# S5 rows ordered (input, place), and the input product's operand built on the vector engine from broadcast rows

## The chip, the cores and the metric

The kernel runs on one core of a Trainium2 chip. The metric is device time of one execution in microseconds (us); less is better. The engines of the core work side by side, each through its own queue in order: PE (TensorE, matrix products; its weight loads are listed as PEld), DVE (VectorE), ACT (ScalarE), POOL (GpSimd) and SP (SyncE), which here issues nearly all DMAs.

## The reference, cut to what matters

One layer with two kinds of heads in parallel, for a prompt of 256 positions and eight sample sequences of 8 positions, 320 columns in all. The part that the change touches is the S5 head group: 64 groups of 16 channels, each driving a 64-dimensional complex diagonal state.

```python
lam_bar = jnp.exp(lam_dt)
b_bar = ((lam_bar - 1.0) / lam)[..., None] * b
bu = jnp.einsum('nlgh,gph->lngp', ug, b_bar)
a = jnp.broadcast_to(lam_bar, (l, 1, S5_GROUPS, S5_STATE))
_, xs = lax.associative_scan(_lin_combine, (a, bu), axis=0)
y = jnp.einsum('lngp,ghp->nlgh', xs, c).real.reshape(n, l, S5_WIDTH)
y = y + d * uf
```

Around it stand the input projection (u, and q, k, v, g of eight retention heads), chunked retention with a per-head norm, a GLU on the S5 output, the output projection, and a SwiGLU feed-forward block with its norms.

## The kernel before

All activations are held transposed (features on partitions, 320 columns). Large products run in a helper `gemm` (L137): per 128-row step `k` three matmuls of 320 columns, high x high, high x low and low x high (L143 to L145), from weights that `wload` (L122) brings in slabs of eight steps: one DMA into `raw` on SP (L130), a cast to `hi` on ACT (L131), and `lo = raw - hi` on DVE (L133), three buffers of each.

The order on PE and POOL is written out by the program (`manual_schedule`, L924). DVE, ACT and SP are ordered by a planner: among what is ready it takes what was traced first, and a block under `high_priority(offset=...)` counts as that much earlier (weights 3000, evictions `EVAC` 1500). Each engine then works through its queue in order. Small work is woven between the projection's steps by generators: `clk.now` is a clock that counts 0.4 for each `k` step (L146), the given costs in `mm` (L101) and 0.12 for a transpose in `tr` (L105). A generator that says `yield DL["b1"]` goes on when the clock has moved that far (`run_due`, L91). The distances stand in `DL` (L918).

S5 runs in eight chunks `c` of eight groups. Chunk `c` starts at clock `T0 + PER * c` (L990, L920), chunk 0 out of the first head's value step (`head_v`, L748). A chunk handles four positions (`CH = 4`) at once, so one product takes rows (position in the block, channel). In `s5_chunk` (L583), in order:

- the chunk's columns `up_` go to DRAM (`via`) and come back as `kst`, whose 64-row halves are ordered (place, input channel): eight DMAs (L593 to L596);
- on DVE, `m1`, `m2` are B times the coefficients `gpc` (and C times `lpc`), then `bl` and `cl` are the real and imaginary combinations (L606 to L619), and the table `tb` (`s5_table`, L525);
- after `b1`: four transposes of `bl` on PE into a PSUM bank `pt` (L626 to L628), copied on ACT to `bst` (L630), and the load of the next but one chunk's B and C (`load_bc`, L547);
- after `b2`: the input product `pb` (32 matmuls, `bst` x `kst`, L639), the product `pk_` (16 matmuls), whose result goes to the last place of `toe`, and six DMAs that shift it to the other places (L650 to L653); then the scan on DVE (`s5_scan`, L552);
- after `scan`: the output product `py` (16 matmuls `toe` x `kst`, 32 `cl` x `xp`, L659 to L674), its eviction `ev`, one DMA to DRAM (`back`, L682) and eight back as `yc` (L684 to L687);
- after `y`: the D term and GELU on DVE and ACT, into `u32`.

`gpc` and `lpc`, the coefficients by chunk, are made once in `s5_powers` (L485) from `ff`, `gp` and `lp`, which `s5_params3` (L439) computes on DVE. In `head_v` the sample part of the values is copied twice on ACT, to `vsp` (L757, for the product of a pair of heads, L774) and to `vs` (L758), which goes to DRAM as `vd` (L1100) during the GLU product.

After the last projection (L1012) the program runs the remaining generators until chunk 7 is done (L1026), and then the products with `w_out` (`ps_o`), the GLU product (`ps_g`), again `w_out`, and the feed-forward block.

Of the kernel before, what the change touches and what calls it, by code (L numbers as in the profile page):

```python
# [12 lines left out]
F32 = mybir.dt.float32  # L13
# [19 lines left out]
CH = 4  # L33
NCP = NP // CH
NC = N // CH
# [6 lines left out]


@with_exitstack
def hybrid_kernel(ctx, tc, xT, w_in, w_in4, w_out, w_glu, w_fi, w_fo, vecs, s5p, bc, x0,
                  r0, trig, masks, kdec, kdf, gq,
                  yT, s5p_o, s5s_o, rp_o, rs_o):
    nc = tc.nc
    pe, act, dve, pool, sp = nc.tensor, nc.scalar, nc.vector, nc.gpsimd, nc.sync
# [18 lines left out]
    vd = drs.tile([H, NS, NB, P], F32, name="vd")  # L68
    voff = {}
    o = 0  # L70
# [30 lines left out]
    def mm(cost, *a, **k):  # L101
        pe.matmul(*a, **k)
        clk.now += cost

    def tr(out, in_):  # L105
        m = in_.shape[0]
        pe.transpose(out, in_, ident[:m, :m])
        clk.now += 0.12
# [68 lines left out]
    def tt(out, a, b, op):  # L177
        dve.tensor_tensor(out, a, b, op)  # L178
        return out
# [63 lines left out]
    def misc(name):  # L243
        return ps_m.tile([P, 512], F32, name=name, tag="misc", bufs=2)
# [8 lines left out]
    vs = mp.tile([64, H, P], F32, name="vs")  # L253
    gqt = mp.tile([P, H, NS], F32, name="gqt")
    retp = mp.tile([P, H, N], F32, name="retp")

# [2 lines left out]
        pool.memset(qgs[i], 0.0)  # L259

    smp = mp.tile([P, P], F32, name="smp")
    vsp = mp.tile([P, P], F32, name="vsp")
# [52 lines left out]
    gpc = s5.tile([P, 8, 2, 8, CH], F32, name="gpc")  # L315
    ecs = s5.tile([P, 2 * NE, NPAIR], F32, name="ecs")
    lx0 = s5.tile([P, 2, NPAIR, NB], F32, name="lx0")
    endp = s5.tile([P, 2, NPAIR], F32, name="endp")
    ends = s5.tile([P, 2, 2, NPAIR, NB], F32, name="ends")

# [164 lines left out]
    def s5_powers():  # L485
        for q in range(2):
            for d in range(2):
                o = lpc[:, :, q, 4 * d:4 * d + 4]
                act.mul(o, lp[:, q].rearrange("p e (c j) -> p c j e", j=4), -1.0 if d > q else 1.0)
                o = gpc[:, :, q, 4 * d:4 * d + 4]  # L490
                act.copy(o[:, :, :, 0], ff[:, q].rearrange("p (c j) -> p c j", j=4))
                act.copy(o[:, :, :, 1:], gp[:, q].rearrange("p e (c j) -> p c j e", j=4))

    def s5_turns(ec, es):
        pool.memset(e18[:, :, 0, :, 0:1], 1.0)
# [87 lines left out]
    def s5_chunk(c):  # L583
# [7 lines left out]
        sp.dma_start(via.rearrange("j g h s c -> (j g h) (s c)"), up_.rearrange("p s c -> p (s c)"))  # L591
        kst = s5.tile([P, 4, NC], F32, name="kst", tag="kst", bufs=2)
        for i in range(2):  # L593
            for e in range(CH):
                sp.dma_start(kst[64 * i + 16 * e:64 * i + 16 * e + 16],
                             via[2 * i:2 * i + 2, :, :, CH - 1 - e].rearrange("q g h c -> h (q g) c"))  # L596

        raw = raws[c]
        for q in range(2):
# [5 lines left out]
        shm = [P, 8, CH, 16]  # L605
        for w_, pc in ((0, gpc), (1, lpc)):  # L606
            m1, m2 = (s5.tile(shm, F32, name=f"m{q}", tag=f"m{q}", bufs=1) for q in range(2))
            b_ = raw[:, w_].unsqueeze(2).to_broadcast(shm)
            tt(m1, b_, pc[:, c, 0].unsqueeze(3).to_broadcast(shm), MUL)
            tt(m2, b_, pc[:, c, 1].unsqueeze(3).to_broadcast(shm), MUL)  # L610
            if w_ == 0:

                bl = s5.tile([P, 2, 2, 2, CH, 16], F32, name="bl", tag="bl", bufs=1)
                for r, (a, b, op) in enumerate(((m1[:, 0:4], m2[:, 4:8], SUB), (m1[:, 4:8], m2[:, 0:4], ADD))):
                    a, b = (t_.rearrange("p (u q) e h -> p u q (e h)", q=2) for t_ in (a, b))
                    tt(bl[:, r].rearrange("p q u e h -> p u q (e h)"), a, b, op)
# [5 lines left out]
        yield DL["b1"] + (4.0 if c == 0 else 0.0)  # L622
        if not c:
            tbl = s5_table(c)
        bst = s5.tile([P, 4, P], F32, name="bst", tag="bst", bufs=1)
        pt = misc("pt")  # L626
        for i in range(4):
            tr(pt[:, P * i:P * i + P], bl[:, i // 2, i % 2].rearrange("p u e h -> p (u e h)"))  # L628
        with tc.high_priority(offset=EVAC):
            act.copy(bst, pt.rearrange("p (i s) -> p i s", s=P))  # L630
        load_bc(c + 2)
        yield DL["b2"]
        pb = ps_b.tile([P, 2, 512], F32, name="pb", tag="pb", bufs=1)
        for i in range(4):
            for u in range(2):

                for g in range(2):
                    us, gs = slice(64 * u, 64 * u + 64), slice(64 * g, 64 * g + 64)
                    mm(0.04, pb[gs, u, NC * i:NC * i + NC], bst[us, i, gs], kst[us, 2 * (i % 2) + g],  # L639
                       start=True, stop=True, tile_position=(64 * u, 64 * g))  # L640
        pk_ = misc("pk_")
        for i in range(2):
            for q in range(2):
                for u in range(2):
                    mm(0.04, pk_[64 * u:64 * u + 64, 32 * i:32 * i + 32],
                       bl[:, q, i, u].rearrange("p e h -> p (e h)"), cl0[:, q, 2 * u + i],
                       start=q == 0, stop=q == 1, tile_position=(0, 64 * u))
        with tc.high_priority(offset=EVAC):
            act.copy(toe[:, :, CH - 1], pk_[:, 0:64].rearrange("p (q h) -> p q h", h=16))
        for u in range(2):  # L650
            for t in range(CH - 1):
                d = 16 * (CH - 1 - t)
                sp.dma_start(toe[64 * u + d:64 * u + 64, :, t], toe[64 * u:64 * u + 64 - d, :, CH - 1])  # L653
        with tc.high_priority(offset=2 * EVAC if c == 7 else 0):
            s5_scan(c, pb, xp, d0, tbl)
        yield DL["scan"]
# [21 lines left out]
            tt(ev, ev,  # L678
               py[:, :, 2 * NC:4 * NC].rearrange("p g (u c) -> p u g c", c=NC), ADD)

        back = drm.tile([2, CH, 16, 2, 2, NC], F32, name="back", tag="back", bufs=2)
        sp.dma_start(back.rearrange("i t h u g c -> (i t h) (u g c)"), ev.rearrange("p u g c -> p (u g c)"))  # L682
        yc = s5.tile([P, CH, NC], F32, name="yc", tag="yc", bufs=1)
        for j in range(4):  # L684
            for g in range(2):
                r = 32 * j + 16 * g
                sp.dma_start(yc[r:r + 16], back[j % 2, :, :, j // 2, g].rearrange("t h c -> h t c"))  # L687
# [60 lines left out]
    def head_v(h, v_, qg, rt, R):  # L748
# [22 lines left out]
        nt = 2 + h % 2  # L771
        if h % 2:
            two = (HS[h - 1], R)
            mm(0.22, po[:, 2], smp, vsp, start=True, stop=False, skip_group_check=True)  # L774
# [133 lines left out]
    def do_g(h):  # L908
        ps = proj(11 + 4 * h)
        sg = mp.tile([P, N], F32, name="sg", tag="sg", bufs=2)  # L910
        with tc.high_priority(offset=EVAC):
# [337 lines left out]
def _host(inp):  # L1249
# [36 lines left out]
    A["bc"] = c(np.stack([np.concatenate([pairs(p + q, p == "s5_c_") for q in ("re", "im")], 2)  # L1286
                          for p in ("s5_b_", "s5_c_")], 2))
    x0 = np.stack([g("state_s5_re")[0], g("state_s5_im")[0]], 0)
    A["x0"] = c(x0.reshape(2, NB, NPAIR, P).transpose(3, 0, 2, 1))
    A["r0"] = c(g("state_ret")[0].transpose(1, 2, 0, 3))  # L1290
# [53 lines left out]
```

## Time and profile before

| | |
|---|---|
| time, median of 3 runs | 1434.91 us (1433.25 to 1435.58) |
| the profiled execution | 1433.95 us, its span 1432.1 us |
| TensorE clock granted | 0.997 |
| ACT, DVE, POOL busy | 598.8, 954.6, 125.1 us |
| DMA | 101803 packets, 266.87 MB, mean 186 GB/s |

The page of the profile gives busy time by engine, then groups of instructions by line, with the number, the mean duration of one, and the idle time of the engine ahead of them. A timeline row is start, duration, engine, line, operation, tiles written and read, and in brackets the idle time before it and what ended it. The duration of a PE matmul overlaps with the next one's, so the distance between two starts is read beside it. SPq rows are DMA issues: their duration is that of the issue, and the landing comes later.

### The profile page before, as it was taken

The page shows a single profiled execution, that of the slowest core. Times are in us where ns is not written, and L with a number is a line of the kernel's source. Part 1 is how long each engine was busy: PE and PEld are TensorE (multiplying, and loading weights), DVE is VectorE, ACT ScalarE, POOL GpSimd, SP SyncE. Part 2 cuts the span into 40 slices and gives each one's busy share as a digit, 9 for nine tenths or more (in the row PEclk, how much of TensorE's full clock was granted, in tenths as well). Part 3 has the DMA queues.
Part 4 walks back from the last instruction along what each step waited for, and adds up shares of the span by engine and source line. Part 5 has one row for each costly group of instructions (what it writes and reads, how often), then busy time and mean ns, then how long its engine had stood idle before and what let it go on. Part 6 is the DMA issues. An engine that isn't in the chain of part 4 may idle for free.

```text
span 1432.1 us, 26209 instructions
## 1 busy us (share of the span) xinstructions
PE 1418.1 (99%) x10394; PEld 1407.6 (98%) x10394; DVE 954.6 (67%) x1853; ACT 598.8 (42%) x944; POOL 125.1 (9%) x193
## 2 busy tenths in 40 slices
PE   9999999999999999999999999999999999999996
PEld 9999999999999999999999999999999999999996
DVE  7978887777567647776677546777644767644554
ACT  7645555554355433333333333333333333333452
POOL 7530022110000010000001000001000000000001
PEclk9999999999999999999999999999999999999998
DMA  8555555556544466675666446757445765444442
GB/s 285 175 172 161 165 167 165 169 160 208 162 156 152 152 210 228 221 250 205 239 217 228 128 150 234 247 202 254 151 152 185 256 225 183 153 127 156 148 148 108
DMA packets 101803, 266.87 MB, mean 186 GB/s; under 512 B 27312, under 2 KB 41776, under 8 KB 101680
## 3 DMA queue, kind: packets, MB, share of 16 engines
q1 hardware_dynamic: 101536, 264.94, 55.7%
q8 instruction: 81, 1.33, 0.4%
q14 instruction: 42, 0.34, 0.1%
q10 hardware_dynamic: 144, 0.26, 0.1%
HBM read 254.24 MB, written 10.52 MB: 185 GB/s over the span
## 4 chain that ended last, share of the span: by engine, by line
PE 71%; DVE 1%; issue 0%; ACT 0%; DVEq 0%
PE ps_fu L144 7%; PE ps_fu L143 7%; PE ps_fo L143 7%; PE ps_fo L144 7%; PE ps_fo L145 7%; PE ps_fu L145 7%; PE ps_fg L144 7%; PE ps_fg L143 7%; PE ps_fg L145 7%; PE ps_o L145 1%; PE ps_o L143 1%; PE ps_o L144 1%; PE ps_g L144 1%; PE ps_g L145 1%; PE ps_g L143 1%; DVE x L178 0%
## 5 line engine op out<-in xcount | busy, mean ns | idle before, releaser
L131 ACT CAST hi<-raw 128x1024 fp32r<-128x1024 f32 (+1 forms) x416 | 402.2, 968 | 697.4 <-PE ps_fo L144 189.0
L133 DVE TENSOR_TENSOR lo<-raw,hi 128x1024 fp32r<-128x1024 f32 (+1 forms) x416 | 467.5, 1124 | 314.9 <-ACT hi L131 312.4
L144 PE MATMUL ps_fo<-alo,hi 128*128 128x320 f32 x704 | 217.5, 309 | 0.0
L143 PE MATMUL ps_fg<-hhi,hi 128*128 128x320 f32 x704 | 217.5, 309 | 0.0
L143 PE MATMUL ps_fo<-ahi,hi 128*128 128x320 f32 x704 | 217.5, 309 | 0.0
L145 PE MATMUL ps_fo<-ahi,lo 128*128 128x320 f32 x704 | 217.5, 309 | 0.0
L144 PE MATMUL ps_fu<-hlo,hi 128*128 128x320 f32 x704 | 217.4, 309 | 0.0
L145 PE MATMUL ps_fg<-hhi,lo 128*128 128x320 f32 x704 | 217.4, 309 | 0.0
L143 PE MATMUL ps_fu<-hhi,hi 128*128 128x320 f32 x704 | 217.4, 309 | 0.0
L144 PE MATMUL ps_fg<-hlo,hi 128*128 128x320 f32 x704 | 217.4, 309 | 0.0
L145 PE MATMUL ps_fu<-hhi,lo 128*128 128x320 f32 x704 | 217.4, 309 | 0.0
L143 PE MATMUL ps_p<-xhi,hi 128*128 128x320 f32 x560 | 177.3, 317 | 0.0
L145 PE MATMUL ps_p<-xhi,lo 128*128 128x320 f32 x560 | 173.0, 309 | 0.0
L144 PE MATMUL ps_p<-xlo,hi 128*128 128x320 f32 x560 | 172.8, 309 | 0.0
L144 PEld LDWEIGHTS ps_fg<-hlo,hi 128*128 128x128 f32 x704 | 132.4, 188 | 0.0
L143 PEld LDWEIGHTS ps_fo<-ahi,hi 128*128 128x128 f32 x704 | 132.4, 188 | 0.0
L143 PEld LDWEIGHTS ps_fu<-hhi,hi 128*128 128x128 f32 x704 | 132.4, 188 | 0.0
L144 PEld LDWEIGHTS ps_fu<-hlo,hi 128*128 128x128 f32 x704 | 132.4, 188 | 0.0
L145 PEld LDWEIGHTS ps_fo<-ahi,lo 128*128 128x128 f32 x704 | 132.4, 188 | 0.0
L145 PEld LDWEIGHTS ps_fu<-hhi,lo 128*128 128x128 f32 x704 | 132.4, 188 | 0.0
L143 PEld LDWEIGHTS ps_fg<-hhi,hi 128*128 128x128 f32 x704 | 132.3, 188 | 0.0
L145 PEld LDWEIGHTS ps_fg<-hhi,lo 128*128 128x128 f32 x704 | 132.3, 188 | 0.0
(441 smaller groups left out, 2066.6 us busy)
## 6 DMA issues: line engine op xcount, KB each, us to landing
raw<-w_fi SPq DMA_DIRECT2D x176, 512.0 KB, 4.1
raw<-w_in SPq DMA_DIRECT2D x79, 512.0 KB, 4.1
raw<-w_fo SPq DMA_DIRECT2D x64, 512.0 KB, 3.5
raw<-w_out SPq DMA_DIRECT2D x32, 512.0 KB, 3.7
hi<-vd SPq DMA_DIRECT2D x32, 512.0 KB, 5.5
lo<-vd SPq DMA_DIRECT2D x32, 512.0 KB, 5.2
raw<-w_fo SPq DMA_DIRECT2D x64, 192.0 KB, 2.4
rt<-r SPq DMA_DIRECT2D x8, 512.0 KB, 5.3
```

The costliest lines, as they stand in the source:

```text
L131: cast = act.copy(hi[:, :m], raw[:, :m])
L133: last_lo[0] = dve.tensor_tensor(lo[:, :m], raw[:, :m], f(hi[:, :m]), SUB)
L143: pe.matmul(ps, hi, xhi[:, k], start=k == 0, stop=False)
L144: pe.matmul(ps, hi, xlo[:, k], start=False, stop=False)
L145: pe.matmul(ps, lo, xhi[:, k], start=False, stop=k == nk - 1)
```

## The change

Rows of the S5 operands are ordered (input channel, place) in place of (place, input channel). With that order `kst` comes from DRAM in two DMAs of 64 rows, `yc` in four of 32 rows, and `back` is written in four; `toe` is shifted by six DMAs over every fourth partition.

The transposed operand of the input product is no longer made by transposing `bl`. The host passes B already in rows, once for each of the four places (`bt`). A new generator `s5_rows` copies the coefficients into `gs` (eight ACT copies), transposes them once (two PE transposes), and writes them to DRAM (`gtd`). For each chunk `load_rows` loads `btr` (256 KB) and, broadcast over the 16 inputs, `gtr` (two DMAs of 128 KB), and `s5_bst` multiplies them on DVE: six operations of 128x256. `bl` stays, for `pk_`. `load_rows(c + 1)` stands behind chunk `c`'s `pb`.

`vs` gets the pair layout of `vsp`, which goes; `vd` is written by sixteen DMAs in place of eight.

```diff
@@ s5_powers
-                o = gpc[:, :, q, 4 * d:4 * d + 4]
-                act.copy(o[:, :, :, 0], ff[:, q].rearrange("p (c j) -> p c j", j=4))
-                act.copy(o[:, :, :, 1:], gp[:, q].rearrange("p e (c j) -> p c j e", j=4))
+            for e in range(CH):
+                src = gp[:, q, e - 1] if e else ff[:, q]
+                act.copy(gpc[:, :, q, :, CH - 1 - e].rearrange("p c (d j) -> p c d j", j=4),
+                         src.rearrange("p (c j) -> p c j", j=4).unsqueeze(2).to_broadcast([P, 8, 2, 4]))
+
+    def s5_rows():
+
+        gs = s5.tile([P, 2, 2, CH, 8, 2], F32, name="gs", tag="bl", bufs=1)
+        for r in range(2):
+            for e in range(CH):
+                src = gp[:, r, e - 1] if e else ff[:, r]
+                act.copy(gs[:, r, :, CH - 1 - e], src.rearrange("p (c u q) -> p u c q", u=2, q=2))
+        yield DL["rows"]
+        pt = misc("pt")
+        for r in range(2):
+            tr(pt[:, P * r:P * r + P], gs[:, r].rearrange("p u e c q -> p (u e c q)"))
+        gt = s5.tile([P, 2, P], F32, name="gt", tag="gtr", bufs=1)
+        with tc.high_priority(offset=EVAC):
+            act.copy(gt, pt[:, 0:2 * P].rearrange("p (r s) -> p r s", s=P))
+        sp.dma_start(gtd.rearrange("u e c q r s -> (u e c q) (r s)"), gt.rearrange("p r s -> p (r s)"))
+        load_rows(0)
+
+    rows = {}
+
+    def load_rows(c):
+        if c < 8:
+            b, g = (s5.tile([P, 2, 2, P], F32, name=n, tag=n, bufs=1) for n in ("btr", "gtr"))
+            sp.dma_start(b, bt[c])
+            for u in range(2):
+                sp.dma_start(g[64 * u:64 * u + 64].rearrange("p q r s -> p (q r s)"),
+                             gtd[u, :, c].rearrange("e q r s -> e (q r s)").unsqueeze(0)
+                             .to_broadcast([16, CH, 4 * P]))
+            rows[c] = b, g
+
+    def s5_bst(c):
+        b, g = rows.pop(c)
+        t_ = s5.tile([P, 2, 2, P], F32, name="bt_", tag="m0", bufs=1)
+        for r in range(2):
+            tt(t_[:, :, r], b[:, :, 1 - r], g[:, :, 1], MUL)
+        for r in range(2):
+            tt(b[:, :, r], b[:, :, r], g[:, :, 0], MUL)
+            tt(b[:, :, r], b[:, :, r], t_[:, :, r], ADD if r else SUB)
+        return b
@@ s5_chunk
-            for e in range(CH):
-                sp.dma_start(kst[64 * i + 16 * e:64 * i + 16 * e + 16],
-                             via[2 * i:2 * i + 2, :, :, CH - 1 - e].rearrange("q g h c -> h (q g) c"))
+            sp.dma_start(kst[64 * i:64 * i + 64], via[2 * i:2 * i + 2].rearrange("q g h s c -> (h s) (q g) c"))
...
-        bst = s5.tile([P, 4, P], F32, name="bst", tag="bst", bufs=1)
-        pt = misc("pt")
-        for i in range(4):
-            tr(pt[:, P * i:P * i + P], bl[:, i // 2, i % 2].rearrange("p u e h -> p (u e h)"))
-        with tc.high_priority(offset=EVAC):
-            act.copy(bst, pt.rearrange("p (i s) -> p i s", s=P))
+        bst = s5_bst(c).rearrange("p q r s -> p r q s")
         load_bc(c + 2)
         yield DL["b2"]
...
+        load_rows(c + 1)
...
-        for u in range(2):
-            for t in range(CH - 1):
-                d = 16 * (CH - 1 - t)
-                sp.dma_start(toe[64 * u + d:64 * u + 64, :, t], toe[64 * u:64 * u + 64 - d, :, CH - 1])
+        for t in range(CH - 1):
+            for i in range(t + 1):
+                sp.dma_start(toe[i::CH, :, t], toe[i + CH - 1 - t::CH, :, CH - 1])
...
-        back = drm.tile([2, CH, 16, 2, 2, NC], F32, name="back", tag="back", bufs=2)
-        sp.dma_start(back.rearrange("i t h u g c -> (i t h) (u g c)"), ev.rearrange("p u g c -> p (u g c)"))
+        back = drm.tile([2, CH, 2, 2, 16, NC], F32, name="back", tag="back", bufs=2)
+        for u in range(2):
+            for g in range(2):
+                sp.dma_start(back[:, :, u, g].rearrange("i t h c -> (i t) h c"), ev[:, u, g])
         yc = s5.tile([P, CH, NC], F32, name="yc", tag="yc", bufs=1)
         for j in range(4):
-            for g in range(2):
-                r = 32 * j + 16 * g
-                sp.dma_start(yc[r:r + 16], back[j % 2, :, :, j // 2, g].rearrange("t h c -> h t c"))
+            sp.dma_start(yc[32 * j:32 * j + 32], back[j % 2, :, j // 2].rearrange("t g h c -> (g h) t c"))
@@ head_v
-        act.copy(vsp[64 * (h % 2):64 * (h % 2) + 64], vT[64:128, 2])
-        last = act.copy(vs[:, h], vT[64:128, 2])
+        last = act.copy(vs[64 * (h % 2):64 * (h % 2) + 64, h // 2], vT[64:128, 2])
         if h == 0:
             rot_t["values"] = last
             with tc.issue_after(last.ins):
                 s5_powers()
+                spawn(s5_rows())
             start_chunk(0)
@@ DL
-    DL = dict(b1=14.2, b2=6.6, scan=17.8, y=10.0, k=8.5, v=6.1,
+    DL = dict(b1=14.2, b2=6.6, scan=17.8, y=10.0, rows=11.0, k=8.5, v=6.1,
@@ the GLU product
-            sp.dma_start(vd[:, :, n].rearrange("h t e -> t h e"), vs[NS * n:NS * n + NS])
+            for g in range(2):
+                sp.dma_start(vd[g::2, :, n].rearrange("h t e -> t h e"), vs[64 * g + NS * n:64 * g + NS * n + NS])
```

More of the change, by code (lines that the diff above doesn't have):

```diff
@@ L44, in hybrid_kernel @@
 @with_exitstack
-def hybrid_kernel(ctx, tc, xT, w_in, w_in4, w_out, w_glu, w_fi, w_fo, vecs, s5p, bc, x0,
+def hybrid_kernel(ctx, tc, xT, w_in, w_in4, w_out, w_glu, w_fi, w_fo, vecs, s5p, bc, bt, x0,
                   r0, trig, masks, kdec, kdf, gq,
@@ L261, in hybrid_kernel @@
     smp = mp.tile([P, P], F32, name="smp")
-    vsp = mp.tile([P, P], F32, name="vsp")
     qsp = mp.tile([P, P], F32, name="qsp")
@@ L317, in hybrid_kernel @@
     lx0 = s5.tile([P, 2, NPAIR, NB], F32, name="lx0")
+    gtd = drm.tile([2, CH, 8, 2, 2, P], F32, name="gtd", tag="gtd", bufs=1)
     endp = s5.tile([P, 2, NPAIR], F32, name="endp")
@@ L604, in s5_chunk @@
             act.copy(d0[:, :, :, 1:], r4[:, js].unsqueeze(1).unsqueeze(3).to_broadcast([P, 2, 4, NCP - 1]))
-        shm = [P, 8, CH, 16]
         for w_, pc in ((0, gpc), (1, lpc)):
+            dm = 3 - w_
+            shm = [P, 8, CH, 16] if w_ else [P, 8, 16, CH]
             m1, m2 = (s5.tile(shm, F32, name=f"m{q}", tag=f"m{q}", bufs=1) for q in range(2))
-            b_ = raw[:, w_].unsqueeze(2).to_broadcast(shm)
-            tt(m1, b_, pc[:, c, 0].unsqueeze(3).to_broadcast(shm), MUL)
-            tt(m2, b_, pc[:, c, 1].unsqueeze(3).to_broadcast(shm), MUL)
+            b_ = raw[:, w_].unsqueeze(dm).to_broadcast(shm)
+            tt(m1, b_, pc[:, c, 0].unsqueeze(5 - dm).to_broadcast(shm), MUL)
+            tt(m2, b_, pc[:, c, 1].unsqueeze(5 - dm).to_broadcast(shm), MUL)
             if w_ == 0:
-                bl = s5.tile([P, 2, 2, 2, CH, 16], F32, name="bl", tag="bl", bufs=1)
+                bl = s5.tile([P, 2, 2, 2, 16, CH], F32, name="bl", tag="bl", bufs=1)
                 for r, (a, b, op) in enumerate(((m1[:, 0:4], m2[:, 4:8], SUB), (m1[:, 4:8], m2[:, 0:4], ADD))):
-                    a, b = (t_.rearrange("p (u q) e h -> p u q (e h)", q=2) for t_ in (a, b))
-                    tt(bl[:, r].rearrange("p q u e h -> p u q (e h)"), a, b, op)
+                    a, b = (t_.rearrange("p (u q) h s -> p u q (h s)", q=2) for t_ in (a, b))
+                    tt(bl[:, r].rearrange("p q u h s -> p u q (h s)"), a, b, op)
                 continue
@@ L638, in s5_chunk @@
                     us, gs = slice(64 * u, 64 * u + 64), slice(64 * g, 64 * g + 64)
-                    mm(0.04, pb[gs, u, NC * i:NC * i + NC], bst[us, i, gs], kst[us, 2 * (i % 2) + g],
+                    mm(0.04, pb[gs, u, NC * i:NC * i + NC], bst[us, i // 2, i % 2, gs], kst[us, 2 * (i % 2) + g],
                        start=True, stop=True, tile_position=(64 * u, 64 * g))
+        load_rows(c + 1)
         pk_ = misc("pk_")
@@ L773, in head_v @@
             two = (HS[h - 1], R)
-            mm(0.22, po[:, 2], smp, vsp, start=True, stop=False, skip_group_check=True)
+            mm(0.22, po[:, 2], smp, vs[:, h // 2], start=True, stop=False, skip_group_check=True)
             for j in range(4):
@@ L1287, in _host @@
                           for p in ("s5_b_", "s5_c_")], 2))
+    bt = np.stack([pairs("s5_b_" + q, False) for q in ("re", "im")], 0)
+    bt = bt.reshape(2, P, 8, 2, 2, 16).transpose(2, 3, 5, 4, 0, 1)
+    A["bt"] = c(np.broadcast_to(bt[:, :, :, None], (8, 2, 16, CH, 2, 2, P)).reshape(8, P, 2, 2, P))
     x0 = np.stack([g("state_s5_re")[0], g("state_s5_im")[0]], 0)
```

4 lines of the change are left out of this document (2 added, 2 removed).

## The prediction

> **What bounds the kernel now.** The first view is the page's table of busy time, then the same shares over the stretch in which the S5 chunks run.
>
> ```profile
> span 1432.1 us, 26209 instructions
> ...
> PE 1418.1 (99%) x10394; PEld 1407.6 (98%) x10394; DVE 954.6 (67%) x1853; ACT 598.8 (42%) x944; POOL 125.1 (9%) x193
> ```
>
> ```profile
> 43.50:341.90 298.40, 297.87 (x2750) 290.90 (x2748) 243.12 (x516) 162.48 (x360) 63.23 (x114) 1.00 0.52 161
> ```
>
> The columns of the second are stretch, length, then busy us and instructions of PE, PEld, DVE, ACT and POOL, granted clock, DMA share and GB/s. From the first projection after the norm to the last, PE stands still for 298.40 - 297.87 = 0.53 us. DVE has 55.3 us left there, ACT 136. So an instruction taken off PE is worth its slot, and one put on DVE is free until PE has to wait for it. What PE waited for is the third view.
>
> ```profile
> PE py L102 <- DMA toe<-toe: 0.5, 1, 0.5
> ...
> PE pss L102 <- POOL ksp L886: 0.5, 1, 0.5
> PE ps_g L144 <- DVE ylo L182: 0.3, 1, 0.3
> ```
>
> Columns: total us, times, longest. No wait is for `kst` or `yc`: fewer DMAs as such can win back only the 0.5 us of `toe`.
>
> **Off PE: 32 transposes.** The timeline of PE around chunk 0's four, and their group:
>
> ```profile
> 78.29 0.31 PE L145 MATMUL ps_p<-xhi,lo 128*128 128x320 f32 x1
> 78.44 0.60 PE L107 MATMUL pt<-ident,bl 128*128 128x128 f32 x4
> 78.79 0.39 PE L143 MATMUL ps_p<-xhi,hi 128*128 128x320 f32 x1
> 79.03 0.30 PE L144 MATMUL ps_p<-xlo,hi 128*128 128x320 f32 x1
> ```
>
> ```profile
> L107 PE MATMUL pt<-ident,bl 128*128 128x128 f32 x32 | 4.8, 272 | 0.0
> ```
>
> Instructions overlap, so the price is the distance of starts. The next projection matmul begins 78.79 - 78.44 = 0.35 us after the first transpose, and the one after it follows 0.24 us later instead of the usual 0.15, which costs 0.09 more. One group is 0.44 us, eight are 3.5. `s5_rows` puts two transposes back: one start distance of (0.60 - 0.272) / 3 = 0.11, a short one and the 0.09, about 0.2. **Net on PE: -3.3 us.** The products `pb`, `pk` and `py` keep their number and shapes.
>
> The Trainium skill ("TensorE: Matmul & The Clock Gate", Part 4: PE-mode transpose) gives about 275 ns for a transpose inside a kernel and says that access latency dominates it. The group's mean of 272 ns agrees as a duration; the start of the next matmul after 0.35 us for four does not agree as a price.
>
> **Onto DVE: six operations of 128x256 a chunk. Off ACT: the copy of `bst`.** Nearest rows, in the views by form:
>
> ```profile
> L178 DVE TENSOR_TENSOR bl<-m,m 128x256 f32<-128x256 f32 x16 | 6.2, 420 | 0.2
> ```
>
> ```profile
> L630 ACT COPY bst<-pt 128x512 f32<-128x512 f32 x8 | 4.7, 588 | 0.4 <-PE pt L107 0.4
> ...
> L492 ACT COPY gpc<-gp 128x96 f32<-128x96 f32 x4 | 0.9, 299 | 0.0
> ```
>
> DVE gets 6 x 0.42 = 2.5 us a chunk, 20.2 in all, against 55.3 idle. ACT loses 4.7 us and the eight copies into `vsp`, and gains eight copies of 32 elements into `gs` (each under the 299 ns of the 96-element copy) and one of `gt`: a gain on an engine with 136 us to spare, worth nothing. In chunks 1 to 7 `btr` and `gtr` are ordered right behind the previous chunk's `pb`, some 33 us ahead, and the six operations follow `tb`, which is done ahead of its chunk's transposes; there I price the new wait of `pb` at nothing. The cover is the 6.6 units of the planner between the old transposes and `pb` (8.5 us in chunk 0, 78.44 to 86.96); without it a chunk would cost up to 2.5 us. Bounds for the 20.2 us of DVE work: nothing, or 20.2 if none were hidden; I take nothing outside chunk 0, since the idle time is the nearer row. The reordered products `m`, `bl` keep shapes and counts; their new strides I take at 0, by the rows of the same shape.
>
> **DMAs.** Per chunk `kst` goes from 8 to 2, `yc` from 8 to 4, `back` from 1 to 4, `toe` stays at 6, and three loads (256 + 2 x 128 KB) come in: 25 become 21.
>
> ```profile
> kst<-via SPq DMA_DIRECT2D x64, 20.0 KB, 3.4
> back<-ev SPq DMA_DIRECT2D x8, 160.0 KB, 3.6
> yc<-back SPq DMA_DIRECT2D x64, 20.0 KB, 3.5
> raw_bc<-bc SPq DMA_DIRECT2D x8, 128.0 KB, 3.7
> ```
>
> ```profile
> L595 SPq DMA_DIRECT2D kst<-via x64: 306/424/1315, 47.8 to 319.2; - x64
> ```
>
> ```profile
> L653 SPq DMA_DIRECT2D toe<-toe x48: 585/597/1404, 88.7 to 340.7; - x48
> ```
>
> The first fence ends in us to landing, the other two give ns of issue (least, median, most). SP saves 10 issues of about 0.42 us and pays 3 more `back` and 3 loads, so some 1.7 us a chunk, if the larger `kst` issues at the same price (at the 0.6 of `toe` still 1.3). No wait of PE hangs on it, except at two places.
>
> **Place 1, chunk 7's second product.** PE's order is fixed in the program: `py` of chunk 7 stands right behind the last projection and ahead of the `w_out` products.
>
> ```profile
> 330.04 0.78 PE L102 MATMUL pb<-kst,bst 64*64 64x80 f32 x32
> ```
>
> ```profile
> 341.95 0.36 PE L102 MATMUL py<-kst,toe 64*64 64x80 f32 x4
> 342.80 0.43 PE L102 MATMUL py<-kst,toe 64*64 64x80 f32 x10 [0.50 <-DMA toe<-toe]
> ```
>
> ```profile
> 332.34 1.37 SPq L687 DMA_DIRECT2D yc<-back  x3
> 333.80 1.88 SPq L653 DMA_DIRECT2D toe<-toe  x3
> 338.29 0.36 SPq L130 DMA_DIRECT2D raw<-w_out  x1
> 338.75 2.54 SPq L653 DMA_DIRECT2D toe<-toe  x3
> ```
>
> ```profile
> 337.04 1.22 DVE L133 TENSOR_TENSOR lo<-raw,hi 128x1024 fp32r<-128x1024 f32 x1
> 338.18 0.75 DVE L178 TENSOR_TENSOR xp<-v,v 128x252 f32<-128x252 f32 x2
> ```
>
> Chunks start at fixed readings of the planner's clock, which counts 0.4 for a projection step that takes 0.44 us. Without 3.1 units of transposes by then, 8 to 9 more steps fit ahead of `pb`(7): it moves to about 330.7, while the last projection ends 3.3 us earlier and PE reaches `py` at 338.65. The distance that hid the scan and `toe` shrinks from 11.9 to 8.0 us. `xp` is ready 8.9 us after `pb` (338.93), so at 339.6: PE reaches the products that read it near 339.1 and waits 0.5, as long as before. `toe`: half of its DMAs stood behind a weight load that waited for `lo` until 338.26, and three `yc` stood ahead of it. Now `yc` has 4 DMAs and `kst`(7) only 2, so `yc`(6) should be through before `toe` is ready near 332.4. Six issues of 0.6 end at 336.3; with the last landing about 1.5 us behind its issue (342.80 against 338.75 + 2.54) that is 337.8, in time. I take a wait of 0.5 us here, change 0; bounds: -0.5 and +4.0 (rival A).
>
> **Place 2, chunk 0's operand**, which needs the coefficient rows through DRAM first.
>
> ```profile
> 54.29 0.55 PE L107 MATMUL pst<-ident,v__743 128*128 128x128 f32 x3
> ```
>
> ```profile
> 64.75 0.91 ACT L492 COPY gpc<-gp 128x96 f32<-128x96 f32 x4
> ```
>
> ```profile
> 70.06 0.35 SPq L130 DMA_DIRECT2D raw<-w_in  x1
> ...
> 73.46 0.33 SPq L130 DMA_DIRECT2D raw<-w_in  x1
> ...
> 78.87 6.05 SPq L130 DMA_DIRECT2D raw<-w_in  x3
> ```
>
> ```profile
> 76.95 0.76 DVE L178 TENSOR_TENSOR tb<-e,e 128x256 f32<-128x256 f32 x2
> ...
> 80.64 1.75 DVE L133 TENSOR_TENSOR lo<-raw,hi 128x1024 fp32r<-128x1024 f32 x1
> 83.09 1.48 DVE L133 TENSOR_TENSOR lo<-raw,hi 128x1024 fp32r<-128x1024 f32 x1 [0.69 <-ACT hi L131]
> 86.19 0.42 DVE L178 TENSOR_TENSOR sm<-pss,mk 128x256 f32<-128x256 f32 x1 [1.62 <-PE pss L102]
> ```
>
> ```profile
> 86.96 0.78 PE L102 MATMUL pb<-kst,bst 64*64 64x80 f32 x32
> ```
>
> The rows' two transposes stand 11 units behind head 0's value transposes: 11 / 0.4 x 0.44 = 12.1 us and some products of the head, so near 68. Their input `gs` comes after the `gpc` copies, near 67: a wait of PE of 0 to 1.5 us, I take 0. Then a copy, `gtd` out (landing 3.6 as `back`) and `gtr` in (3.7 as `raw_bc`), each behind a weight load: about 69.5, 73.5, 77.5. The six operations then have 9 us, in which DVE is idle for 0.69 + 1.62 us and has 2.5 to do: `pb`(0) is late by 0.2, which I take.
>
> The sum: -3.3 + 0 + 0.2 = **-3.1 us**, so a profiled execution of 1433.95 - 3.1 = 1430.9 with a span near 1429.0 (1.9 us lie around the span). That execution lies 0.96 below the median of the three runs; against the median it is 1434.9 - 3.1 = **1431.8 us**. About 0.2%, 2.9 us, is what a measurement of this kernel can tell from no change, so the forecast lies just beyond it.
>
> **Rivals.**
>
> A. *The end of the projections is bound by chunk 7, not by PE.* If a weight load splits `toe` as before, its last half lands at 342.80 + 0.7 = 343.5 while PE is at `py` from 338.65; after the first products it waits 4.5 us instead of 0.5. Sum: -3.3 + 4.0 = +0.7, **1435.6**. For it: the split and the shrunken distance; against: the fewer DMAs ahead. Chance 0.22.
>
> B. *The rows come late, slower than before.* DVE works in order: a `bst` operation that waits for `gtr` holds the `lo` of the weights behind it. If `gtr` is issued behind the three weight loads that keep SP from 78.87 to 84.92, it lands near 88.5; 2.5 us of products, with a `lo` of 1.22 between, bring `pb`(0) to 92.5 instead of 86.96, and the held `lo` adds about 1: +6.5 in all, **1438.1**. It decides from rows landing after 83, and costs more than it wins from about 86. For it: DVE is full here, and `lo` took 1.75 and 1.48 instead of 1.22 while Pool worked. Chance 0.13.
>
> The Trainium skill ("SBUF — State Buffer", SBUF: two separate sides) says that a DVE instruction with two SBUF inputs and a GpSimd instruction that reads SBUF exclude each other for the whole instruction. All six operations have two SBUF inputs; the `lo` of 1.75 us agrees in direction, and by it the 2.5 us would be 3.6 (x 1.75 / 1.22), by the rule more: chunk 0 would be a microsecond or two later, on rival B's side.
>
> C. *DVE becomes a bound in stretches.* Its 20.2 us make 263 of 298; 0.4 us of lateness a chunk in `lo` or an eviction undoes the gain: 8 x 0.4 = 3.2, **1434.8**. For it, the stretch ahead of chunk 0's product:
>
> ```profile
> 60.00:80.00 20.00, 20.00 (x140) 19.99 (x139) 19.44 (x48) 11.64 (x23) 11.02 (x18) 1.00 0.51 164
> ```
>
> DVE is busy for 19.44 of 20 us there. Against it: PE has no wait on DVE in the whole stretch. Chance 0.12.
>
> D. *A transpose costs its whole duration.* 30 x 0.272 = 8.2 us, **1426.7**. Against it: the 0.35 us to the next start. Chance 0.05. (The rule of the Trainium skill on PE-mode transposes, quoted above, leads to this figure.)
>
> **How the numbers follow.** Forecast 0.48, A 0.22, B 0.13, C 0.12, D 0.05. Faster by over 0.2%: 0.36 of the forecast's 0.48 and D, 0.41. Within: 0.12 of the forecast, 0.16 of A, C: 0.40. Slower: 0.06 of A and B: 0.19. The range goes from 1430.3 (both half-microsecond waits gone, a fast median) to 1438.0, leaving out D and the worse half of B.
>
> **What would show it.** Right: PE busy near 1415, 30 fewer L107 matmuls, PE waits within 1.5 us in all. Wrong at place 1: a PE wait for `toe` or `xp` of over 2 us near 339. Wrong at place 2: a PE wait for DVE at chunk 0's `pb`, or for ACT at the rows' transposes. C: waits for `lo` spread over chunks. A wait for `btr` or `gtr` in chunks 1 to 7 would break the claim that they come early.

## The result, and the profile after

| | before | after |
|---|---|---|
| time, median of 5 runs each | 1434.84 us (1433.25 to 1435.58) | 1448.99 us (1445.60 to 1450.28) |
| ratio | | 1.0098 [1.0086, 1.0109] |
| profiled execution, its span | 1433.95, 1432.1 us | 1450.28, 1448.5 us |
| TensorE clock granted | 0.997 | 0.992 |

The kernel became 1% slower where the forecast was 0.2% faster. First the table of busy time of the kernel after, from its page, and the stretch that the prediction read (stretch, length, then busy us and instructions of PE, PEld, DVE, ACT and POOL, clock, DMA share, GB/s):

```profile
span 1448.5 us, 26168 instructions
...
PE 1422.7 (98%) x10364; PEld 1409.0 (97%) x10364; DVE 972.7 (67%) x1901; ACT 592.8 (41%) x937; POOL 121.7 (8%) x193
```

```profile
43.50:341.90 298.40, 292.25 (x2637) 282.83 (x2638) 250.43 (x542) 152.02 (x342) 62.01 (x114) 0.99 0.56 169
```

PE has 30 instructions fewer, as forecast, but stands still for 298.40 - 292.25 = 6.2 us in a stretch where it stood still for 0.5. PE's waits (total us, times, longest):

```profile
PE py L102 <- ACT hi L131: 5.2, 1, 5.2
PE pss L102 <- POOL ksp L920: 3.1, 2, 2.2
PE ps_p L145 <- DVE lo L133: 1.7, 4, 0.7
...
PE ps_p L143 <- ACT hi L131: 0.8, 1, 0.8
...
PE py L102 <- DVE xp L178: 0.5, 1, 0.5
```

The largest stands at place 1 of the prediction, and 2.2 us of the second stand beside place 2. Together these five are 11.3 us; before, the waits for `toe` and `ksp` were 1.0. The clock costs more, as an estimate from its mean: (1 - 0.992) x 1448.5 = 11.6 us against 4.3. Waits +10.3, clock +7.3, transposes -3.3 make 14.3 of the 16.4 us between the spans; the rest I put down to the rounding of the clock (a thousandth is 1.4 us) and to shorter pauses.

No wait of PE in this list names the cause. That shows in the groups of DVE. The first instruction after the output's way through DRAM, `y1` (`y<-u,vec,yc`, the D term), of before and then of after; the last field is the idle time ahead of it:

```profile
L182 DVE SCALAR_TENSOR_TENSOR y<-u,vec,yc 128x320 f32<-128x320 f32 x8 | 6.3, 788 | 0.0
```

```profile
L182 DVE SCALAR_TENSOR_TENSOR y<-u,vec,yc 128x320 f32<-128x320 f32 x8 | 6.3, 782 | 25.7 <-DMA yc<-back 25.7
```

DVE stands still for 25.7 us for `yc`, in six of the eight chunks, and never did before. The timeline of DVE around chunk 0's `y1`, before and then after (start, duration):

```profile
121.37 0.42 DVE L178 TENSOR_TENSOR t<-pb,tb 128x256 f32<-128x256 f32 x1
...
122.11 1.08 DVE L178 TENSOR_TENSOR t<-pb,tb 128x256 f32<-128x256 f32 x3
...
124.02 1.22 DVE L571 TENSOR_TENSOR_SCAN w<-d,w 128x512 f32<-128x512 f32 x1
...
127.58 0.78 DVE L182 SCALAR_TENSOR_TENSOR y<-u,vec,yc 128x320 f32<-128x320 f32 x1
```

```profile
126.30 0.42 DVE L178 TENSOR_TENSOR t<-pb,tb 128x256 f32<-128x256 f32 x1
128.76 0.79 DVE L182 SCALAR_TENSOR_TENSOR y<-u,vec,yc 128x320 f32<-128x320 f32 x1 [2.04 <-DMA yc<-back]
129.47 0.74 DVE L178 TENSOR_TENSOR t<-pb,tb 128x256 f32<-128x256 f32 x2
...
132.67 1.22 DVE L611 TENSOR_TENSOR_SCAN w<-d,w 128x512 f32<-128x512 f32 x1
```

Before, chunk 0's `y1` stood behind chunk 1's scan. After, the planner has put it into the midst of the `t` operations that lead to that scan. The copy `ev` that starts the trip, before and after:

```profile
112.50 0.42 ACT L677 COPY ev<-py 128x320 f32<-128x320 f32 x1
```

```profile
117.48 0.42 ACT L711 COPY ev<-py 128x320 f32<-128x320 f32 x1
```

The trip from the end of `ev` to `y1` takes 128.76 - 117.90 = 10.9 us after; DVE was free 2.04 us earlier, at 8.8. Before, DVE came to `y1` 127.58 - 112.92 = 14.7 us behind `ev`, so the trip had time to spare. The trip with the new DMAs isn't longer, it is asked for sooner: where `y1` waits for chunk 0's trip with the old DMAs (run x11 below), it begins 13.4 us behind `ev`.

At the end it meets PE. SP, ACT, DVE and PE of the kernel after, from 328 us on:

```profile
328.67 0.38 SPq L849 DMA_DIRECT2D rp_o<-rp  x1
336.18 2.57 SPq L718 DMA_DIRECT2D back<-ev  x4
338.85 0.40 SPq L130 DMA_DIRECT2D raw<-w_out  x1
339.36 0.84 SPq L721 DMA_DIRECT2D yc<-back  x2
...
340.76 0.90 SPq L721 DMA_DIRECT2D yc<-back  x2
```

```profile
334.16 1.16 ACT L838 ACTIVATE on<-po,gy 128x128 f32<-128x128 f32 x3 [6.75 <-POOL gy L832]
335.20 0.43 ACT L711 COPY ev<-py 128x320 f32<-128x320 f32 x1
...
349.70 0.19 ACT L684 COPY toe<-pk__4734 128x64 f32<-128x64 f32 x1
```

```profile
347.91 0.78 DVE L182 SCALAR_TENSOR_TENSOR y<-u,vec,yc 128x320 f32<-128x320 f32 x1 [5.67 <-DMA yc<-back]
348.62 1.21 DVE L133 TENSOR_TENSOR lo<-raw,hi 128x1024 fp32r<-128x1024 f32 x1
349.75 1.41 DVE L178 TENSOR_TENSOR t<-pb,tb 128x256 f32<-128x256 f32 x4
```

```profile
341.64 0.78 PE L102 MATMUL pb<-kst,btr 64*64 64x80 f32 x32
...
355.49 0.81 PE L102 MATMUL py<-kst,toe 64*64 64x80 f32 x16 [5.24 <-ACT hi L131]
```

PE delivers chunk 7's `pb` at 342.42. DVE could read it then, but stands at chunk 6's `y1` until 347.91; ACT's copy into `toe` comes at 349.70, behind the `y1` arithmetic in ACT's queue. PE's own order leaves it only `py`, and it waits 5.24 us (the row names `hi`; what `py` reads are `toe` and `kst`). Chunk 6's `yc` in turn is late because `ev` stood behind an instruction of ACT that waited 6.75 us, and `back` behind `ev`: between 329.05 and 336.18 SP issues nothing, no weights either.

### The profile page after: what moved, and what is told of

It reads as the page before. It is cut to its first block, busy times and chain, and to the rows that moved or that the text cites. A ratio compares the mean times of both kernels' runs of the same rounds, so it can differ in the third digit from the quotient of the medians.

```text
span 1448.5 us, 26168 instructions
## 1 busy us (share of the span) xinstructions
PE 1422.7 (98%) x10364; PEld 1409.0 (97%) x10364; DVE 972.7 (67%) x1901; ACT 592.8 (41%) x937; POOL 121.7 (8%) x193
## 4 chain that ended last, share of the span: by engine, by line
PE 70%; DVE 1%; issue 0%; ACT 0%; DVEq 0%
PE ps_fu L145 7%; PE ps_fu L144 7%; PE ps_fo L144 7%; PE ps_fo L145 7%; PE ps_fo L143 7%; PE ps_fu L143 7%; PE ps_fg L145 7%; PE ps_fg L144 7%; PE ps_fg L143 7%; PE ps_o L145 1%; PE ps_o L143 1%; PE ps_o L144 1%; PE ps_g L144 1%; PE ps_g L145 1%; PE ps_g L143 1%; DVE x L178 0%
```

## The experiments

Four theories were tested. **Theory 1**: the six products make DVE late. **Theory 2**: the new DMAs hold SP's queue and starve the weights. Neither takes the wait of `y1` into account. **Theory 3**: DVE's fixed queue has `y1` ahead of the next chunk's scan, and what stands behind it is late. **Theory 4**, the rival of 3: the three row loads hold SP, and the place of `y1` is incidental. All runs, with two distances from their traces: the idle time ahead of `y1` (all chunks), and the time from the end of chunk 7's `pb` to its first `t` on DVE (1.0 us before, 7.3 after):

| run | what | us | ratio to before | `y1` idle | `pb` to `t` |
|---|---|---|---|---|---|
| x1 | new order and DMAs, transposes kept | 1437.24 | 1.0021 [1.0012, 1.0030] | 13.1 | 3.5 |
| x2 | before, the new operand alone | no time | | | |
| x3 | after, no products on DVE | 1441.33 | 1.0050 [1.0038, 1.0062] | 21.9 | 5.8 |
| x4 | before, six more DVE operations a chunk | 1435.64 | 1.0008 [0.9999, 1.0017] | 0.1 | 1.0 |
| x5 | after, old `back` and `yc` | 1431.09 | 0.9979 [0.9969, 0.9988] | 0.3 | 1.4 |
| x6 | after, `y1` behind the scan | 1431.96 | 0.9990 [0.998, 1.0] | 0.0 | 1.5 |
| x7 | before, new `back` and `yc` | 1439.01 | 1.0032 [1.0020, 1.0045] | 12.0 | 3.4 |
| x8 | x1, `y1` behind the scan | 1433.53 | 0.9994 [0.9985, 1.0003] | 1.5 | 1.0 |
| x9 | x6, chunk 0's operand by transposes | 1430.91 | 0.9976 [0.9966, 0.9986] | 0.0 | 1.4 |
| x10 | after, once more | 1448.89 | 1.0095 [1.0080, 1.0111] | 25.5 | 6.1 |
| x11 | before, `y1` ahead of the scan | 1441.32 | 1.0048 [1.0036, 1.0061] | 2.6 | 7.4 |
| x12 | after, only chunk 6's `y1` behind | 1445.71 | 1.0082 [1.0070, 1.0094] | 24.5 | 3.9 |
| x13 | after, only chunks 0 to 5's `y1` behind | 1440.08 | 1.0033 [1.0021, 1.0045] | 3.5 | 5.1 |

x2 has no time: with the rows' tiles added, the kernel before needs 71.7 KB a partition for its S5 tiles, where 71 are left. So the new operand without the new order of the rows was not measured.

**x1, the order of the rows without the new operand.** `kst`, `bl`, `toe`, `back`, `yc` and `vs` as in the change, without `s5_rows`, `load_rows` and `s5_bst`. Against the kernel after:

```diff
-        bst = s5_bst(c).rearrange("p q r s -> p r q s")
+        bst = s5.tile([P, 4, P], F32, name="bst", tag="bst", bufs=1)
+        pt = misc("pt")
+        for i in range(4):
+            tr(pt[:, P * i:P * i + P], bl[:, i // 2, i % 2].rearrange("p u h s -> p (u h s)"))
+        with tc.high_priority(offset=EVAC):
+            act.copy(bst, pt.rearrange("p (i s) -> p i s", s=P))
```

> The change without its operand: the row order (input, place), the DMAs of the change for kst, back, yc, toe and vd, and the pair layout of vs; the operand again by four transposes and an ACT copy, so no btr, gtr and none of the six DVE operations. Theory 1 (the six DVE operations a chunk make DVE late, and its fixed order turns that into PE waits): about the time before, 1434.8 within 1.5 us. Theory 2 (the new DMAs, with back in four issues behind ev, hold SP's queue and starve the weights): near the changed kernel, 1446 to 1450.

2.4 us over the middle of theory 1's figure, 0.9 beyond its bound, and far from theory 2's: the order of the rows with its DMAs costs 0.2%, not 1%. Neither theory names the 13.1 us ahead of `y1`.

**x3, the products left out, the loads kept.**

```diff
-            tt(t_[:, :, r], b[:, :, 1 - r], g[:, :, 1], MUL)
...
-            tt(b[:, :, r], b[:, :, r], g[:, :, 0], MUL)
-            tt(b[:, :, r], b[:, :, r], t_[:, :, r], ADD if r else SUB)
```

> The changed kernel with the six DVE operations of every chunk left out: the operand is B's rows without the coefficients. The loads of btr and gtr stay. Theory 1: the time that I forecast for the change, 1431.8 within 1 us, with PE waits of less than 1.5 us between 43 and 345 us. Theory 2: still above 1443.

Between both. Without a single product of the 20 us, 7 us of loss remain, so theory 1 is not the whole cause, and theory 2 asked for more. The other 7.7 us did go with the products. Chunk 0 has a part in that: the profile of the kernel after lost 2.2 us there in waiting for `ksp` and, as an estimate from the windows further down, 3.4 to the clock; this one lost neither.

**x4, the products alone, in the kernel before.**

```diff
+        spare = s5.tile([P, 2, 2, P], F32, name="spare", tag="m0", bufs=1)
+        for i in range(6):
+            tt(spare[:, i % 2].rearrange("p q s -> p (q s)"), b0, b1_, MUL)
```

> The kernel before, with six operations of 128x256 with both inputs in SBUF added on DVE in each chunk, where the change has its own; their result is not used, and PE, ACT, SP and all DMAs stay. Theory 1: it shows most of the loss, 1443 or more, with waits of PE for lo and at the end of the projections. Theory 2: 1434 to 1437.

20 us more on DVE cost 1.3 us, all of it at chunk 0 (PE waits 1.1 us for `ksp` and 0.8 for `lo`). The products alone, then, do not make the loss. Theory 2's figures allow this run, but it missed x1 and x3. What is left in DVE's rows is the idle time ahead of `y1`: theory 3.

**x5, the output's way through DRAM as before.**

```diff
-        back = drm.tile([2, CH, 2, 2, 16, NC], F32, name="back", tag="back", bufs=2)
-        for u in range(2):
-            for g in range(2):
-                sp.dma_start(back[:, :, u, g].rearrange("i t h c -> (i t) h c"), ev[:, u, g])
+        back = drm.tile([2, CH, 16, 2, 2, NC], F32, name="back", tag="back", bufs=2)
+        sp.dma_start(back.rearrange("i t h u g c -> (i t h) (u g c)"), ev.rearrange("p u g c -> p (u g c)"))
...
-            sp.dma_start(yc[32 * j:32 * j + 32], back[j % 2, :, j // 2].rearrange("t g h c -> (g h) t c"))
+            for g in range(2):
+                r = 32 * j + 16 * g
+                sp.dma_start(yc[r:r + 16], back[j % 2, :, :, j // 2, g].rearrange("t h c -> h t c"))
```

> The kernel after with one edit undone: the output goes to DRAM and back as before (one back, eight yc); all else stays, the three row loads a chunk too. Theory 3: the time goes where y1, which reads yc, stands in DVE's fixed queue ahead of the next chunk's scan and waits there for yc (25.7 us of idle DVE in the kernel after, none before). Here the queue has y1 behind or beside the scan in most chunks, so y1 waits under 8 us in all, and 1438 to 1443 us are expected; chunk 0's 4.6 us stay. Theory 4: the row loads hold SP's queue and with it the weights, whatever y1 does: 1446 us or more.

7 us better than theory 3 asked for: one more DMA a chunk, and the kernel is 18 us faster than after, with all row loads and products in it. Theory 4 falls. In chunks 2 to 5 `y1` still stands ahead of the scan, but by 1.2 to 2.3 us only, where the kernel after has it 7 to 9 us ahead, and it waits for 0.3 us in all. Chunk 0's loss, which the expectation took as fixed, is gone too.

**x6, the order of DVE alone.**

```diff
-        dve.tensor_tensor_scan(wf, d0.rearrange("p r j t -> p (r j t)"), wf, 0.0, MUL, ADD)
+        s5_state["scan"] = dve.tensor_tensor_scan(wf, d0.rearrange("p r j t -> p (r j t)"), wf, 0.0, MUL, ADD)
...
-    DL = dict(b1=14.2, b2=6.6, scan=17.8, y=10.0, rows=11.0, k=8.5, v=6.1,
+    DL = dict(b1=14.2, b2=6.6, scan=17.8, y=16.0, rows=11.0, k=8.5, v=6.1,
...
-        stt(y1.rearrange("p (c s) -> p c s", s=CH), u32[:, c].rearrange("p (c s) -> p c s", s=CH),
-            v("d", c), yc.rearrange("p s c -> p c s"), MUL, ADD)
+        with tc.issue_after(s5_state["scan"].ins):
+            stt(y1.rearrange("p (c s) -> p c s", s=CH), u32[:, c].rearrange("p (c s) -> p c s", s=CH),
+                v("d", c), yc.rearrange("p s c -> p c s"), MUL, ADD)
```

> The kernel after with one thing moved: y1 is ordered behind the next chunk's scan on DVE, as in the kernel before. No DMA and no operation is added or removed. Theory 3: y1 waits under 2 us in all, PE's wait at chunk 7's second product (5.2 us) falls under 1.5 us, and what stays is chunk 0: 1436.5 us (1435 to 1439). Theory 4: 1445 us or more.

The deciding run. Nothing is added or taken; `y1`, with the arithmetic behind it, is pinned behind the scan and asked for 6 units later, and 17 us are gone. The waits are as expected; the time lies 3 us below its range, which had chunk 0's loss in it; this profile shows none there. DVE and PE at chunk 7:

```profile
332.49 1.41 DVE L178 TENSOR_TENSOR t<-pb,tb 128x256 f32<-128x256 f32 x4
...
336.25 0.76 DVE L182 SCALAR_TENSOR_TENSOR y<-u,vec,yc 128x320 f32<-128x320 f32 x1
...
339.26 0.75 DVE L178 TENSOR_TENSOR xp<-v,v 128x252 f32<-128x252 f32 x2
```

```profile
330.26 0.78 PE L102 MATMUL pb<-kst,btr 64*64 64x80 f32 x32
...
338.80 0.51 PE L102 MATMUL py<-kst,toe 64*64 64x80 f32 x16
339.82 0.98 PE L102 MATMUL py<-xp,cl 64*64 64x80 f32 x32 [0.51 <-ACT hi L131]
```

`t` starts 1.5 us behind `pb`, and PE waits 0.51 us in place of 5.24 + 0.48.

**x7, that part of the change alone**: the edit of x5 the other way round, in the kernel before.

> The kernel before with one part of the change: back in four DMAs and yc in four. No row loads, no products on DVE. Its DVE queue has y1 ahead of the next chunk's scan in all chunks. Theory 3: y1 waits 10 to 25 us in all, and the time is 1436 to 1441 us. Theory 4: 1434.3 +- 1 us.

As theory 3 has it. This one pair of DMA lists moves `y1` in the planner's order, with no other part of the change present.

**x8, x1 with the edit of x6.**

> The new order of the rows with its DMAs, transposes kept, and y1 ordered behind the next chunk's scan. Theory 3: y1 waits under 1 us; with the transposes still on PE the time is that of before, 1434.3 us (1433 to 1436), against 1432.0 with the new operand and 1437.2 with y1 where the planner put it. If the fewer DMAs have a worth of their own: under 1433.

The time is as expected and the interval holds 1; the 1.5 us ahead of `y1` (under 1 was expected) are all in chunk 7, behind which no scan follows. So the new order and its fewer DMAs are worth nothing that this run can tell from 0.

**x9, x6 without products and rows in chunk 0.**

```diff
-        bst = s5_bst(c).rearrange("p q r s -> p r q s")
+        if c:
+            bst = s5_bst(c).rearrange("p q r s -> p r q s")
+        else:
+            bst = s5.tile([P, 2, 2, P], F32, name="btr", tag="btr", bufs=1)
+            pt = misc("pt")
+            for i in range(4):
+                tr(pt[:, P * i:P * i + P], bl[:, i // 2, i % 2].rearrange("p u h s -> p (u h s)"))
+            with tc.high_priority(offset=EVAC):
+                act.copy(bst.rearrange("p r q s -> p (r q) s"), pt.rearrange("p (i s) -> p i s", s=P))
...
-        load_rows(0)
```

> As the run with y1 behind the scan, and chunk 0's operand is made by four transposes as before, so that no rows and no products on DVE are needed there. Theory 3, with chunk 0's loss put down to its products and rows: 1431.5 us (1430 to 1433.5), faster than before by about the 2.8 us that the prediction counted for the transposes. Theory 4: 1442 us or more. If chunk 0's loss has another cause: 1435 to 1439 us.

As expected, and with x5 the fastest, 0.24% below before. Its nine times lie within 1430.57 to 1431.87; the eleven of x6 fall in two groups, six from 1430.16 to 1431.96 and five from 1434.55 to 1436.61. The next run offers a reason.

**x10, the kernel after once more.**

> The kernel after, unchanged, once more. In the profiled execution PE lost 4.6 us around chunk 0, where POOL's kvf took 4.05 us; in two runs whose DVE queue is the same up to there, kvf took 0.43 us and nothing was lost. If that loss is one of single executions, this profile may lack it, and the fastest times are near 1445 and the slowest near 1450 us. If the loss belongs to this program, the profile shows kvf near 4 us again. 1449 us (1445 to 1450.5).

This profile lacks chunk 0's loss (span 1442.2 against 1448.5), and its execution is the fastest of the five (1443.98 to 1451.36). The same instruction of POOL in the first profile of after, in x10 and in x13 (start, duration):

```profile
83.43 4.05 POOL L918 TENSOR_TENSOR kvf<-k__1155,kdt 128x64 f32<-128x64 f32 x1 [4.04 <-DVE k__1155 L178]
```

```profile
82.94 0.44 POOL L918 TENSOR_TENSOR kvf<-k__1155,kdt 128x64 f32<-128x64 f32 x1 [2.70 <-DVE k__1155 L178]
```

```profile
83.39 4.05 POOL L923 TENSOR_TENSOR kvf<-k__1155,kdt 128x64 f32<-128x64 f32 x1 [4.04 <-DVE k__1155 L178]
```

The first two are two executions of one program: 4.05 or 0.44 us. Where it is long, `ksp` behind it and PE's `pss` are late; PE in the first profile of after:

```profile
87.71 0.49 PE L102 MATMUL pss<-qsp,ksp 128*128 128x128 f32 x2 [2.21 <-POOL ksp L920]
```

**x11, the reverse of x6, in the kernel before.**

```diff
-                tt(t[q][:, :, us], pvs[u][:, :, :, 0:NCP], tb[q][:, :, us], MUL)
+                if c:
+                    with tc.issue_after(s5_state["y1"].ins):
+                        tt(t[q][:, :, us], pvs[u][:, :, :, 0:NCP], tb[q][:, :, us], MUL)
+                else:
+                    tt(t[q][:, :, us], pvs[u][:, :, :, 0:NCP], tb[q][:, :, us], MUL)
...
-        stt(y1.rearrange("p (c s) -> p c s", s=CH), u32[:, c].rearrange("p (c s) -> p c s", s=CH),
+        s5_state["y1"] = dve.scalar_tensor_tensor(y1.rearrange("p (c s) -> p c s", s=CH), u32[:, c].rearrange("p (c s) -> p c s", s=CH),
...
-    DL = dict(b1=14.2, b2=6.6, scan=17.8, y=10.0, k=8.5, v=6.1,
+    DL = dict(b1=14.2, b2=6.6, scan=17.8, y=4.0, k=8.5, v=6.1,
```

> The kernel before, with one thing moved: y1 is ordered ahead of the next chunk's first scan operation on DVE. No DMA, layout or operation is changed. Theory 3: y1 waits for yc in most chunks, 15 to 30 us in all, and the time is 1438 to 1447 us. Theory 4, for which the place of y1 is incidental: 1434.3 +- 1 us.

The time is as expected: with every DMA and operation of before, the order alone costs 0.48%. The wait is not: 2.6 us ahead of `y1`, not 15 to 30. The planner filled the queue ahead of `y1` with other work, and DVE waited there, here for PE:

```profile
337.36 0.49 DVE L178 TENSOR_TENSOR sg<-ps_p,rbc 128x320 f32<-128x320 f32 x1 [3.10 <-PE ps_p L145]
...
339.89 0.77 DVE L695 SCALAR_TENSOR_TENSOR y<-u,vec,yc 128x320 f32<-128x320 f32 x1
340.58 1.41 DVE L178 TENSOR_TENSOR t<-pb,tb 128x256 f32<-128x256 f32 x4
```

What did stay is the lateness of the scan: chunk 7's `pb` ends at 333.17 and `t` starts at 340.58. PE's longest wait is again at chunk 7's second product, 2.9 us, here for `xp`. So the idle time ahead of an instruction is no measure of what it holds back; the 7.4 us are.

**x12 and x13, the edit of x6 for some chunks only** (`c == 6`, and `c < 6`).

> The kernel after with y1 ordered behind the next scan for chunk 6 alone, so that only chunk 7's scan is freed. If the loss is that of the last chunk, where PE's own order leaves it nothing else to do, the wait at py falls under 1.5 us and the time to 1440 us (1437 to 1444). If it is the sum of all chunks: 1446 us or more.

> The complement: y1 behind the next scan for chunks 0 to 5, while chunk 6's y1 stays ahead of chunk 7's scan. If the last chunk makes the loss: the wait at py stays at 3 to 5 us, and 1443 us (1440 to 1447). If the lateness of chunk 7 is handed on from the chunks before it: py waits under 1.5 us and the time is 1432 to 1436 us.

x12 falls between its two figures, 0.3 us under that for a sum over all chunks, and PE waits 1.8 + 1.05 us at `py`. x13 lies at the low end of the first, with a wait of 3.0 at `py`. The loss is neither the last chunk's alone nor handed on whole: with chunk 6 alone freed 13.7 us over x6 remain, with chunks 0 to 5 freed 8.1 (of which chunk 0's `kvf`, 4.05 us in that profile, is a part). How a late chunk makes the next one late, by way of `back` in SP's queue, is read from the rows above and wasn't tried by itself.

**What stays open: the size.** The order alone costs 4.4 us in x7 and 6.7 in x11, not the 17 that it costs in the kernel after. The rows and products add nothing where `y1` is late (x8 1433.5, x6 1432.0) and 11.8 us where it is early (x1 1437.2, after 1449.0), 4.1 of them with the row loads (x3), the rest with the products. In chunks 3 to 5 the first `back` is issued 5.6 to 6.5 us behind `ev` in the kernel after, 2.5 to 4.5 without the products (x3), 2.8 to 3.9 in x7, 2.1 to 4.7 in x6. So the products do seem to cost something where DVE also stands still for `y1`; no run takes the two apart.

## Why the prediction was wrong

- **What bounds the kernel: right.** PE did, and its waits carry the loss.
- **Transposes, -3.3 us: right.** Chunk 7's `py` was to begin at 338.65 in place of 341.95. In x6 it begins at 338.80, -3.15. In x8, with the transposes kept, the row is

```profile
341.76 0.51 PE L102 MATMUL py<-kst,toe 64*64 64x80 f32 x16
```

and so -0.2. The price by distances of starts held; rival D, the whole duration (-8.2), did not.
- **Six operations on DVE hidden in chunks 1 to 7: right for the order that the prediction had in mind.** x4 shows it from the one side, x5, x6 and x9 from the other; with `y1` early the products are not free (x3). Rival C, DVE a bound in stretches, showed its sign, waits for `lo` of 1.7 us in several chunks, but not its cause: they are gone in x6 with the same DVE work.
- **DMAs, "No wait of PE hangs on it, except at two places": this step failed.** It counted issues on SP and landings, and took the order of DVE and ACT for given. But they are ordered by a planner, and `back` and `yc` in eight DMAs in place of nine made it place `y1` ahead of the next scan, on a trip that takes 10.9 us. That cost, which the sum put at nothing, is the result: x5 and x6 both remove it (17.9 and 17.0 us), x7 and x11 bring about a part of it alone (4.4 and 6.7). One size was low as well: the four `back` issues take 2.57 us, not the 1.6 or so counted.
- **Place 1: right without that step.** `pb` at 330.7 was forecast, x6 has 330.26 (3.1 units at 0.4 are 7.75 projection steps, not the 8 to 9 of the forecast, and the difference is about one step); `xp` at 339.6, x6 340.01; a wait of 0.5, x6 0.51. In the kernel after it was 5.7, beyond the bound of +4.0. Rival A named the place, not the cause: `toe` wasn't split by weight loads, its source was late, behind `y1`.
- **Place 2: `pb` right, its neighbour missed.** PE waits 0.3 us for `btr` in x6 where 0.2 was forecast. That the products beside POOL's `kvf` could make `pss` late had no price: the prediction named that the two engines shut each other out, but as a cost for DVE. In the first profile of after the six products took 0.41 us or less each, and POOL waited. It comes in some executions; the two groups of x6, some 4 us apart, fit it, though no profile of the later group was taken. Rival B had the chunk and nearly the size (6.5 us; 2.2 of waiting and an estimated 3.4 of clock in the first profile of after), not the mechanism: the rows did not come late.

The forecast sum, 1431.8 us, is near what x6 measures (1431.96), so the terms that were priced held, and the missing one was the order. The agreement to 0.2 us is luck in part: that median is the last of x6's lower group, and the mean of its eleven times is 1433.1.

## What to carry to other kernels

Where a planner orders the queues, any edit of a transfer's shape can move its consumer in an engine's queue: after predicting what is added and removed, ask which instructions read the data, what stands behind them, and how long the trip takes on the chip (here 10.9 us against the 8.8 that the order left). If a consumer isn't urgent, pin it behind the urgent work (doing so with `y1` was worth 17 us). In a trace, look for an idle engine off the bound whose waits are new, since PE's own waits named `hi`, `ksp`, `lo` and `xp`, never `y1` or `yc`; and read the distance from producer to consumer beside it, since other work can fill the wait (x11).

## What the runs showed of the hardware

**A short pause of PE can halve its clock for longer than the pause.** Windows of the kernel after, around chunk 0's wait of 2.21 us and the 5.24 us at `py` (columns as above):

```profile
86.00:88.00 2.00, 0.29 (x3) 0.29 (x3) 1.30 (x2) 0.00 (x0) 1.66 (x2) 1.00 0.86 283
88.00:90.00 2.00, 2.00 (x37) 1.67 (x36) 0.82 (x3) 0.00 (x0) 0.00 (x0) 0.53 0.80 204
90.00:92.00 2.00, 2.00 (x27) 1.77 (x22) 1.52 (x5) 0.68 (x3) 0.00 (x0) 0.50 0.93 313
92.00:94.00 2.00, 2.00 (x9) 2.00 (x8) 0.80 (x1) 1.64 (x4) 0.00 (x0) 0.50 0.35 101
94.00:96.00 2.00, 2.00 (x13) 1.96 (x13) 1.97 (x5) 0.73 (x3) 0.00 (x0) 0.77 0.13 12
```

```profile
355.40:358.00 2.60, 2.03 (x48) 1.80 (x48) 2.60 (x6) 1.56 (x5) 0.00 (x0) 0.50 0.26 68
358.00:361.00 3.00, 3.00 (x19) 2.88 (x12) 3.00 (x7) 0.89 (x2) 0.00 (x0) 0.50 0.97 335
```

Half the clock for some 6 us, after either pause, is 3 us of work more, as an estimate. Pauses of this size don't always do it: after 2.25 us in x13 the clock was 0.53 for 3.5 us only, after 1.89 in x1 0.52 for 3.5 us, and after 1.79 in x7 it stayed at 1.00. The Trainium skill ("TensorE: Matmul & The Clock Gate", Part 1: The HAM clock gate) puts the fall after an idle window of about 3.4 us; here a wait of 2.21 us was enough.

**POOL beside DVE.** `kvf` took 4.05 us where DVE ran `bt_`, `btr` and `lo`, all with two inputs from SBUF, without a pause, and ended at 87.48, with the last `lo` of that run (86.08 + 1.21 = 87.29). The Trainium skill ("SBUF — State Buffer", SBUF: two separate sides) says that such DVE instructions and a GpSimd instruction that reads SBUF exclude each other for the whole instruction; the 4.05 us agree, and the cost falls on whoever waits for POOL. In x10 the same DVE operations ran as densely and `kvf` took 0.44 us, so it can also slip in; what decides it is not shown.
